# Norms of a two-phase transformer kernel: gated rows kept in PSUM, the last half block in two pieces, first features taken straight from the bank

## The chip, the cores and the metric

The kernel runs on one core of a Trainium2 chip. The metric is device microseconds of one execution, as the median of several runs. The names of the engines are those of the profile: PE is TensorE (matmul), DVE is VectorE, ACT is ScalarE, POOL is GpSimd, SP is SyncE, whose queue issues most DMAs.

## What is computed

Two transformer stacks run one behind the other on a batch of one with 256 tokens of width 1024, everything in fp32. The first has two layers on the tokens `x` and on a context `ctx` (its second layer needs the context for the scan's state alone). Cut to what the change touches:

```
for l in range(2):                                   # first stack
    ux = modulate(rmsnorm(x, norm1_g[l]), sh1, sc1) @ w_in[l]     # the same for ctx
    mix_x = concat(conformer_conv(ux), rwkv_out(scan(ux)))
    x = x + gt1 * (mix_x @ w_out[l])                 # gt1, gt2: rows of 1024 gates
    x = x + gt2 * swiglu(modulate(rmsnorm(x, norm2_g[l]), sh2, sc2), wg, wu, wd)
    # layer 0: ctx gets the same two steps
x = rmsnorm(x) * final_g
for l in range(2):                                   # second stack
    x = layer_norm(ALPHA * x + 0.5 * swiglu_2(x, ffn1_w13[l], ffn1_w2[l]))
    x = layer_norm(ALPHA * x + mixer(x))
    x = layer_norm(ALPHA * x + 0.5 * swiglu_2(x, ffn2_w13[l], ffn2_w2[l]))
```

## The kernel before

**Tiling.** Tokens lie on the partitions in two blocks of 128, `x[0]` and `x[1]` (written x0 and x1 in the order's rows), each with 1024 columns in SBUF. A product that ends in token-major form is accumulated in four PSUM banks `acc[b][h]` (acc00 to acc11), block b by half h of 512 columns. Matmuls of fp32 accuracy are made of three: data and weights are each kept as a rounded part and a remainder (`wh` and `wl` for weights, `hi` and `lo` for data), and hi·wh, hi·wl and lo·wh are added up. `wsplit` (L346) makes `wh` with a cast on ACT and `wl` with a subtraction on DVE (L341, L342). The first two weight tiles behind each norm are made apart from that: cast on ACT (L364), subtraction on POOL (L365), a `tensor_tensor` of 128x1024 that reads two SBUF tiles.

**Between two products stands a norm.** There are 11 places in which the PE has finished one product and needs the normalised result for the next:

- six in the first stack. `add_gated` multiplies each bank by a row of gates into an SBUF tile T2 (L620) and adds that to `x` (L621); `rms_blocks` squares each half on ACT with a running sum (L416), adds the two sums in a 128x1 instruction on DVE (L418), takes square root (ACT L384) and reciprocal (DVE L385), and scales (ACT L423, DVE L425). They lie at about 381, 683 (both on the context), 808, 1062, 1347 and 1554 us. At the last three nothing else is ready for the PE; at the first three the scan of the other stream and the gates of the next layer (`ada`) run beside it.
- five in the second stack, at about 1756, 1970, 2164, 2358 and 2577 us. `ln` adds ALPHA·x to the bank (DVE L1146), `ln_norm` takes statistics (L394), merges them (L396), and scales block 0 on ACT (L404) and block 1 on DVE (L406). A sixth LayerNorm ends the program.

Behind both, `feature_major` transposes the eight features of both blocks on the PE (L438), block 0 first, into four banks, and evacuates them by the list `EVAC`: "A e 0" is ACT taking feature 0 to an fp32 tile with scale and shift (L454; on DVE L456 and L458), "h" the cast to the rounded part (ACT L460), "l" the remainder (DVE or POOL, L462). The list fixes the order on each engine.

**What sets the order.** `down_last` gives the last tiles of a product (two in the first stack, four in the second) in three parts: all of block 0, then half 0, then half 1 of block 1, so that the norm of block 0 starts early. All else is put in order by a scheduler that simulates the program's time when it is built; it runs over the whole program, and its waits between engines are put in with it.

Of the kernel before, what the change touches and what calls it, by code (L numbers as in the profile page):

```python
# [47 lines left out]
HALF = [slice(0, 512), slice(512, 1024)]  # L48

# [118 lines left out]
def _layout(a):  # L168
# [84 lines left out]
    "A e 0,D e 2,A h 0,D l 0,A e 1,D e 3,A h 1,A h 2,D l 1,A h 3,D l 2,A e 4,D l 3,A h 4,D e 6,P l 4,A e 5,D e 7,"  # L253
    "A h 5,P l 5,A h 6,A h 7,D l 6,D l 7").split(",")]
# [4 lines left out]
class Prog:  # L259
# [128 lines left out]
    def ln_norm(self, x, b, pre):  # L388

        nc = self.nc  # L390
        st = self.tiny([P, 2, 6])
        for h in range(2):
            pre(b, h)
            nc.vector.bn_stats(st[:, h, :], x[:, HALF[h]])  # L394
# [14 lines left out]
    def rms_blocks(self, blocks, keep=False):  # L409
# [3 lines left out]
        ss = [self.tiny([P, 3]) for _ in range(2)]  # L413
        for b in range(2):
            for h in range(2):
                nc.scalar.activation(self.t(self.pool, [P, 512], "sq", bufs=1), blocks[b][:, HALF[h]], AF.Square,  # L416
                                     accum_out=ss[b][:, h : h + 1])
            nc.vector.tensor_add(ss[b][:, 2:3], ss[b][:, 0:1], ss[b][:, 1:2])  # L418
        for b in range(2):
            r = self.rstd_of(ss[b][:, 2:3], 1.0 / D, RMS_EPS, [P, 1])  # L420
# [7 lines left out]
    def feature_major(self, yb, scale, bias, perm=False, new=None, acc=True):  # L428
# [12 lines left out]
        for e, op, f in (EVAC if acc else EVAC1):  # L441
            hi, lo = hs[f // 4][:, f % 4, :], ls[f // 4][:, f % 4, :]
            eng = {"A": nc.scalar, "D": nc.vector, "P": nc.gpsimd}[e]
            with self.tc.issue_after(last[e].ins) if e in last and acc else contextlib.nullcontext():
                if op == "e":
                    ts[f] = t = self.T1([P, T])
# [88 lines left out]
    def down(self, acc, h, w, start, stop, parts=((0, 0), (0, 1), (1, 0), (1, 1))):  # L535

        for b in range(2):
            s = slice(b * P, b * P + P)
            ns = [n for b_, n in parts if b_ == b]
            for a, c in ((0, 0), (0, 1), (1, 0)):  # L540
                for n in ns:
                    last = self.mm(acc[b][n], h[a][:, s], w[c][:, HALF[n]], start and a == 0 and c == 0,
                                   stop and a == 1)
        return last

    def down_last(self, acc, args):
# [3 lines left out]
        for parts in (((0, 0), (0, 1)), ((1, 0),), ((1, 1),)):  # L550
# [63 lines left out]
    def add_gated(self, x, acc, row):  # L614
        nc = self.nc
        for b in range(2):
            for h in range(2):
                s = HALF[h]
                t = self.T2([P, 512])
                nc.vector.tensor_mul(t, acc[b][h], row[:, s])  # L620
                nc.vector.tensor_add(x[b][:, s], x[b][:, s], t)  # L621
# [518 lines left out]
    def ln(self, x, acc, l, i):  # L1140
# [3 lines left out]
        def pre(b, h):  # L1144
            s = HALF[h]
            nc.vector.scalar_tensor_tensor(x[b][:, s], x[b][:, s], ALPHA, acc[b][h], ALU.mult, ALU.add)  # L1146
# [492 lines left out]
```

## Time and profile before

| | us |
|---|---|
| median of 3 runs | 2779.92 |
| lowest, highest | 2776.57, 2785.88 |
| the profiled execution | 2783.58 |
| its span, first to last instruction | 2781.8 |

The mean granted clock of TensorE in the profiled execution is 0.959 of full speed. The PE is busy for 2632.1 us (95% of the span), DVE for 1716.4, ACT for 1327.3 and POOL for 670.2. What an edit at a norm can give is thus looked for in the PE's gaps, and in what ends each gap, not in the busy shares.

### The profile page before, as it was taken

What the parts mean: (1) busy time and instruction counts of PE and PEld (TensorE: products, weight loads), DVE (VectorE), ACT (ScalarE), POOL (GpSimd) and SP (SyncE); (2) the same over time, 40 slices, a digit from 0 to 9 for tenths busy, and PEclk for the clock granted to TensorE, in tenths of its full rate; (3) what the DMA queues carried; (4) which work ended last, traced back from release to release, by engine and by line L of the source; (5) the groups of instructions that cost most, each with busy time, mean ns of one, the idle gap of its engine ahead of it and who ended that gap; (6) DMA issues with size and microseconds to landing.
All of it is one profiled execution on the core that took longest, in us unless ns stands there. A gap on an engine that the chain in (4) does not pass through costs nothing.

```text
span 2781.8 us, 53780 instructions
## 1 busy us (share of the span) xinstructions
PE 2632.1 (95%) x22398; PEld 2291.3 (82%) x22398; DVE 1716.4 (62%) x2703; ACT 1327.3 (48%) x2015; POOL 670.2 (24%) x669
## 2 busy tenths in 40 slices
PE   7889989999889998899899899999999999999998
PEld 4866867888678896866699899889899898889897
DVE  3885778645577555984555655666655655755655
ACT  5523654434565346433544544654544544644543
POOL 0388999920130001384200000010000000100000
PEclk9989989999899999979899999999999999999999
DMA  7345425334323354234355555524555555425653
GB/s 250 109 145 175 147 84 180 132 130 157 117 77 116 136 182 144 95 137 153 117 187 185 194 183 188 193 87 156 182 187 185 182 188 174 166 83 182 205 184 120
DMA packets 118768, 430.71 MB, mean 155 GB/s; under 512 B 13174, under 2 KB 13686, under 8 KB 118524
## 3 DMA queue, kind: packets, MB, share of 16 engines
q1 hardware_dynamic: 118524, 427.28, 45.2%
q8 instruction: 175, 2.87, 0.4%
q14 instruction: 69, 0.57, 0.1%
HBM read 425.13 MB, written 2.10 MB: 154 GB/s over the span
## 4 chain that ended last, share of the span: by engine, by line
PE 78%; DVE 11%; ACT 4%; POOL 3%; issue 2%; DMA 2%; SPq 0%; ACTq 0%; DVEq 0%; POOLq 0%
PE pb L333 33%; PE acc L333 25%; PE ps L333 19%; DVE wl L342 3%; DVE T1c L726 1%; POOL tap L732 1%; DVE S L964 1%; DVE T L962 1%; DMA raw<-in_ada 1%; DVE x L621 1%; ACT wh L341 1%; POOL x L733 1%; PE acc L438 1%; DMA raw<-in_wr 0%; DVE T2b L620 0%
## 5 line engine op out<-in xcount | busy, mean ns | idle before, releaser
L342 DVE TENSOR_TENSOR wl<-raw,wh 128x1024 fp32r<-128x1024 f32 (+1 forms) x654 | 811.9, 1245 | 622.2 <-ACT wh L341 391.7
L341 ACT CAST wh<-raw 128x1024 fp32r<-128x1024 f32 (+1 forms) x654 | 681.9, 1046 | 892.3 <-PE pb L333 345.8
L333 PE MATMUL pb<-xf,wh 128*128 128x256 f32 (+1 forms) x2560 | 486.4, 289 | 12.6 <-ACT T1b L585 4.1
L333 PE MATMUL pb<-S,wh 128*128 128x256 f32 x2560 | 492.0, 289 | 4.8 <-DVE S L631 1.8
L333 PEld LDWEIGHTS pb<-xf,wh 128*128 128x128 f32 (+1 forms) x2560 | 409.8, 194 | 26.7 <-DVE T1b L588 6.6
L333 PEld LDWEIGHTS pb<-S,wh 128*128 128x128 f32 x2560 | 408.5, 192 | 22.4 <-issue 11.8
L333 PE MATMUL ps<-S,wh 128*128 128x256 f32 x2048 | 390.4, 287 | 0.6 <-ACT S L460 0.5
L333 PE MATMUL pb<-xf,wl 128*128 128x256 f32 (+1 forms) x1280 | 371.2, 291 | 8.7 <-DVE wl L342 8.7
L365 POOL TENSOR_TENSOR wl<-raw,wh 128x1024 fp32r<-128x1024 f32 x22 | 54.9, 2504 | 1340.4 <-ACT wh L364 826.9
L333 PE MATMUL pb<-S,wl 128*128 128x256 f32 x1280 | 367.4, 287 | 2.0 <-DVE wl L342 2.0
L333 PEld LDWEIGHTS ps<-S,wh 128*128 128x128 f32 x2048 | 326.8, 192 | 9.0 <-issue 3.4
L333 PE MATMUL ps<-S,wl 128*128 128x256 f32 x1024 | 293.4, 286 | 0.6 <-DVE wl L342 0.6
L333 PEld LDWEIGHTS pb<-xf,wl 128*128 128x128 f32 (+1 forms) x1280 | 248.1, 194 | 16.7 <-DVE wl L342 11.5
L333 PEld LDWEIGHTS pb<-S,wl 128*128 128x128 f32 x1280 | 245.4, 192 | 6.6 <-issue 3.0
L333 PE MATMUL acc<-wh,T 128*128 128x512 f32 x704 | 206.3, 393 | 0.0
L333 PEld LDWEIGHTS ps<-S,wl 128*128 128x128 f32 x1024 | 196.7, 192 | 2.8 <-issue 1.4
L333 PE MATMUL acc<-wh,T1b 128*128 128x512 f32 x528 | 157.5, 396 | 3.5 <-ACT T1b L341 3.5
L732 POOL TENSOR_SCALAR tap<-z,cols 128x255 f32<-128x255 f32 (+14 forms) x120 | 149.2, 1252 | 0.0
L333 PEld LDWEIGHTS acc<-wh,T 128*128 128x128 f32 x704 | 126.9, 189 | 23.6
L732 POOL TENSOR_SCALAR tap<-x,cols 128x246 f32<-128x246 f32 (+6 forms) x104 | 111.4, 1079 | 46.1 <-DVE x L671 46.0
L733 POOL TENSOR_TENSOR x<-x,tap 128x247 f32<-128x247 f32 (+8 forms) x132 | 106.8, 809 | 34.4 <-ACT tap L730 28.0
L733 POOL TENSOR_TENSOR z<-z,tap 128x255 f32<-128x255 f32 (+14 forms) x120 | 112.8, 940 | 3.9
(445 smaller groups left out, 3968.7 us busy)
## 6 DMA issues: line engine op xcount, KB each, us to landing
raw<-in_fu SPq DMA_DIRECT2D x132, 512.0 KB, 3.2
raw<-in_ada SPq DMA_DIRECT2D x96, 512.0 KB, 4.3
raw<-in_pu SPq DMA_DIRECT2D x88, 512.0 KB, 4.2
raw<-in_qu SPq DMA_DIRECT2D x88, 512.0 KB, 3.7
raw<-in_fd SPq DMA_DIRECT2D x66, 512.0 KB, 3.2
raw<-in_wr SPq DMA_DIRECT2D x51, 512.0 KB, 3.6
raw<-in_pd SPq DMA_DIRECT2D x44, 512.0 KB, 4.1
raw<-in_qd SPq DMA_DIRECT2D x44, 512.0 KB, 3.8
```

Of the source, the lines that this page charges most:

```text
L333: return self.nc.tensor.matmul(out, lhsT, rhs, start=start, stop=stop, **kw)
L341: self.nc.scalar.copy(hi, src)
L342: self.nc.vector.tensor_sub(lo, src, hi.bitcast(F32))
L365: self.nc.gpsimd.tensor_sub(lo, r, hi.bitcast(F32))
L438: nc.tensor.transpose(pt[f // 2][:, f % 2, b, :], yb[b][:, f * P : f * P + P], self.cst("ident"))
L621: nc.vector.tensor_add(x[b][:, s], x[b][:, s], t)
L726: nc.vector.scalar_tensor_tensor(av[:, d], z[:, f, s], w(j), av[:, d], ALU.mult, ALU.add)
L732: nc.gpsimd.tensor_scalar(t[:, d], z[:, f, s], w(j), None, ALU.mult)
L733: nc.gpsimd.tensor_add(zc[f][:, d], zc[f][:, d], t[:, d])
L962: nc.vector.tensor_mul(tv, tj[:, k + 1 : 32, k : k + 1].broadcast_to([P, m, k + 1]), X[:, k : k + 1, 0 : k + 1].broadcast_to([P, m, k + 1]))
L964: nc.vector.tensor_sub(X[:, k + 1 : 32, 0 : k + 1], X[:, k + 1 : 32, 0 : k + 1], tv)
```

## The change

Three edits, of which two are in the norms and one in the evacuation.

1. `add_gated` multiplies the bank by the gates in place: the product stays in PSUM, and the add reads `x` from SBUF and the product from PSUM. The tile T2 is gone there.
2. `PIECES` divides the second half of block 1 in two pieces of 256 columns. `down_last` has four parts in place of three, and the matmuls of the last two are 256 columns wide; the gated add, ALPHA·x, the statistics (four of 256 for block 1) and the squares of block 1 follow the pieces. `rms_blocks` has three squares and two small sums for block 1.
3. `EVAC` has the new operation "H": ACT writes the rounded part of features 0 and 1 straight from the bank, while DVE takes the fp32 copy of the same feature. DVE has 12 operations in place of 10, ACT 11 in place of 12, POOL 1 in place of 2.

```diff
+PIECES = HALF, [slice(0, 512), slice(512, 768), slice(768, 1024)]
+
+
+def piece(acc, s):
+
+    return acc[s.start // 512][:, s.start % 512 : s.start % 512 + s.stop - s.start]
...
 EVAC = [t.split() for t in (
-    "A e 0,D e 2,A h 0,D l 0,A e 1,D e 3,A h 1,A h 2,D l 1,A h 3,D l 2,A e 4,D l 3,A h 4,D e 6,P l 4,A e 5,D e 7,"
-    "A h 5,P l 5,A h 6,A h 7,D l 6,D l 7").split(",")]
+    "A H 0,D e 0,D l 0,A H 1,D e 1,A e 2,D l 1,A h 2,D e 3,A h 3,D l 2,A e 4,D l 3,A h 4,D e 6,A e 5,D l 4,A h 5,D e 7,"
+    "P l 5,A h 6,D l 6,A h 7,D l 7").split(",")]
...
     def ln_norm(self, x, b, pre):
 
         nc = self.nc
-        st = self.tiny([P, 2, 6])
-        for h in range(2):
-            pre(b, h)
-            nc.vector.bn_stats(st[:, h, :], x[:, HALF[h]])
+        n = 2 * len(PIECES[b]) - 2
+        st = self.tiny([P, n, 6])
+        for s in PIECES[b]:
+            pre(b, s)
+            for q in range(s.start * n // D, s.stop * n // D):
+                nc.vector.bn_stats(st[:, q, :], x[:, D // n * q : D // n * (q + 1)])
...
-        ss = [self.tiny([P, 3]) for _ in range(2)]
+        ss = [self.tiny([P, 5]) for _ in range(2)]
+        sums = []
         for b in range(2):
-            for h in range(2):
-                nc.scalar.activation(self.t(self.pool, [P, 512], "sq", bufs=1), blocks[b][:, HALF[h]], AF.Square,
-                                     accum_out=ss[b][:, h : h + 1])
-            nc.vector.tensor_add(ss[b][:, 2:3], ss[b][:, 0:1], ss[b][:, 1:2])
+            c = lambda i: ss[b][:, i : i + 1]
+            for i, s in enumerate(PIECES[b]):
+                nc.scalar.activation(self.t(self.pool, [P, 512], "sq", bufs=1)[:, 0 : s.stop - s.start], blocks[b][:, s],
+                                     AF.Square, accum_out=c(i))
+                if i:
+                    nc.vector.tensor_add(c(2 + i), c(i), c(1 + i if i > 1 else 0))
+            sums.append(c(2 + i))
         for b in range(2):
-            r = self.rstd_of(ss[b][:, 2:3], 1.0 / D, RMS_EPS, [P, 1])
+            r = self.rstd_of(sums[b], 1.0 / D, RMS_EPS, [P, 1])
...
-                if op == "e":
-                    ts[f] = t = self.T1([P, T])
+                if op in "eH":
+
+                    t = hi
+                    if op == "e":
+                        ts[f] = t = self.T1([P, T])
...
             for a, c in ((0, 0), (0, 1), (1, 0)):
                 for n in ns:
-                    last = self.mm(acc[b][n], h[a][:, s], w[c][:, HALF[n]], start and a == 0 and c == 0,
-                                   stop and a == 1)
+                    last = self.mm(piece(acc[b], n), h[a][:, s], w[c][:, n], start and a == 0 and c == 0,
+                                   stop and a == 1 and n.stop % 512 == 0)
...
-        for parts in (((0, 0), (0, 1)), ((1, 0),), ((1, 1),)):
+        for parts in ([(0, s) for s in PIECES[0]], *([(1, s)] for s in PIECES[1])):
...
     def add_gated(self, x, acc, row):
         nc = self.nc
         for b in range(2):
-            for h in range(2):
-                s = HALF[h]
-                t = self.T2([P, 512])
-                nc.vector.tensor_mul(t, acc[b][h], row[:, s])
-                nc.vector.tensor_add(x[b][:, s], x[b][:, s], t)
+            for s in PIECES[b]:
+                a = piece(acc[b], s)
+                nc.vector.tensor_mul(a, a, row[:, s])
+                nc.vector.tensor_add(x[b][:, s], x[b][:, s], a)
...
-        def pre(b, h):
-            s = HALF[h]
-            nc.vector.scalar_tensor_tensor(x[b][:, s], x[b][:, s], ALPHA, acc[b][h], ALU.mult, ALU.add)
+        def pre(b, s):
+            nc.vector.scalar_tensor_tensor(x[b][:, s], x[b][:, s], ALPHA, piece(acc[b], s), ALU.mult, ALU.add)
```

The scheduler's simulation comes out otherwise, and with it the order of much of the first stack: before about 1380 us PE, DVE and ACT work of different streams changes places at many points. ACT's table loads are 83 in the order of the changed kernel, 79 in that before. Behind that point the order differs at the norms alone.

Three pieces of the order, in both kernels. The words in brackets name the engines on whose progress an instruction waits ("Activation" is ACT).

DVE at the final RMS norm (1554 us), from the first product of block 1 on; acc10 and acc11 are the halves of block 1, `tnb` are the 128x1 sums. Before:

```order
L620 TENSOR_TENSOR T2b_2960_17188<-acc10_2668_15285,Sb_2655_15254 128x512 [waits DVE_49,PE_49]
L620 TENSOR_TENSOR T2b_2961_17191<-acc11_2669_15286,Sb_2655_15254 128x512 [waits DVE_49,PE_49]
L621 TENSOR_TENSOR x1_68<-x1_68,T2b_2960_17188 128x512 [waits DVE_49]
L621 TENSOR_TENSOR x1_68<-x1_68,T2b_2961_17191 128x512 [waits DVE_49]
L418 TENSOR_TENSOR tnb_2962_17194<-tnb_2962_17194 128x1 [waits Activation_49]
L418 TENSOR_TENSOR tnb_2963_17195<-tnb_2963_17195 128x1 [waits Activation_49]
L385 RECIPROCAL tnb_2968_17206<-tnb_2968_17206 128x1 [waits Activation_49]
L385 RECIPROCAL tnb_2969_17211<-tnb_2969_17211 128x1 [waits Activation_49]
```

and changed:

```order
L636 TENSOR_TENSOR acc10_2655_15326<-acc10_2655_15326,Sb_2642_15295 128x512 [waits PE_49]
L636 TENSOR_TENSOR acc11_2656_15327<-acc11_2656_15327,Sb_2642_15295 128x256 [waits PE_49]
L637 TENSOR_TENSOR x1_68<-x1_68,acc10_2655_15326 128x512 [waits DVE_49]
L637 TENSOR_TENSOR x1_68<-x1_68,acc11_2656_15327 128x256 [waits DVE_49]
L431 TENSOR_TENSOR tnb_2945_17239<-tnb_2945_17239 128x1 [waits Activation_49]
L636 TENSOR_TENSOR acc11_2656_15327<-acc11_2656_15327,Sb_2642_15295 128x256 [waits DVE_49]
L637 TENSOR_TENSOR x1_68<-x1_68,acc11_2656_15327 128x256 [waits DVE_49]
L393 RECIPROCAL tnb_2952_17254<-tnb_2952_17254 128x1 [waits Activation_49]
L431 TENSOR_TENSOR tnb_2946_17240<-tnb_2946_17240 128x1 [waits Activation_49]
L431 TENSOR_TENSOR tnb_2946_17240<-tnb_2946_17240 128x1 [waits DVE_49,Activation_49]
```

The sums of block 0 come between the two pieces of acc11. The first piece of acc11 waits for the PE, the second waits for DVE alone.

ACT at the first LayerNorm (1756 us): S is the scaled block, `wh` the rounded part of the second of the two weight tiles that POOL finishes. Before:

```order
L384 ACTIVATE tn_19195<-tn_19193,const 128x1
L364 CAST wh_19312<-raw_19310 128x1024
L404 ACTIVATE S_19198<-x_67,tn_19199,tn_19195 128x512 x2
L384 ACTIVATE tn_19210<-tn_19208,const 128x1
L454 ACTIVATE T_3296_19240<-acc_3292_19220,cols 128x256
```

and changed:

```order
L392 ACTIVATE tn_19255<-tn_19253,const 128x1
L414 ACTIVATE S_19258<-x_67,tn_19259,tn_19255 128x512 x2
L372 CAST wh_19375<-raw_19373 128x1024
L392 ACTIVATE tn_19273<-tn_19271,const 128x1
L471 ACTIVATE S_19279<-acc_3276_19283,cols 128x256 x2
```

The cast of `wh` stands behind the scaling of block 0 instead of ahead of it; the first two evacuations are now the "H" ones.

DVE at the same norm, from ALPHA·x of block 1's first half on. Before:

```order
L1146 SCALAR_TENSOR_TENSOR x1_68<-x1_68,acc10_2990_17289 128x512 [waits PE_49]
L385 RECIPROCAL tn_3281_19195<-tn_3281_19195 128x1 [waits Activation_49]
L401 SCALAR_TENSOR_TENSOR tn_3283_19199<-tn_3280_19193,tn_3281_19195 128x1 [waits DVE_49]
L394 BN_STATS tn_3284_19203<-x1_68 128x6
L1146 SCALAR_TENSOR_TENSOR x1_68<-x1_68,acc11_2991_17290 128x512 [waits PE_49]
L394 BN_STATS tn_3284_19203<-x1_68 128x6 [waits DVE_49]
L396 BN_AGGR tn_3285_19208<-tn_3284_19203 128x2 [waits DVE_49]
L385 RECIPROCAL tn_3286_19210<-tn_3286_19210 128x1 [waits Activation_49]
L406 TENSOR_SCALAR S_3287_19213<-x1_68,tn_3285_19208,tn_3286_19210 128x512 [waits DVE_49]
L406 TENSOR_SCALAR S_3287_19213<-x1_68,tn_3285_19208,tn_3286_19210 128x512
```

and changed:

```order
L1161 SCALAR_TENSOR_TENSOR x1_68<-x1_68,acc10_2974_17337 128x512 [waits PE_49]
L393 RECIPROCAL tn_3265_19255<-tn_3265_19255 128x1 [waits Activation_49]
L411 SCALAR_TENSOR_TENSOR tn_3267_19259<-tn_3264_19253,tn_3265_19255 128x1 [waits DVE_49]
L404 BN_STATS tn_3268_19263<-x1_68 128x6 x2
L1161 SCALAR_TENSOR_TENSOR x1_68<-x1_68,acc11_2975_17338 128x256 [waits PE_49]
L1161 SCALAR_TENSOR_TENSOR x1_68<-x1_68,acc11_2975_17338 128x256
L404 BN_STATS tn_3268_19263<-x1_68 128x6 [waits DVE_49] x2
L406 BN_AGGR tn_3269_19271<-tn_3268_19263 128x2 [waits DVE_49]
L393 RECIPROCAL tn_3270_19273<-tn_3270_19273 128x1 [waits Activation_49]
L416 TENSOR_SCALAR S_3271_19276<-x1_68,tn_3269_19271,tn_3270_19273 128x512 [waits DVE_49]
L416 TENSOR_SCALAR S_3271_19276<-x1_68,tn_3269_19271,tn_3270_19273 128x512
```

Two steps of 256 columns stand in place of one of 512, and both stand ahead of the statistics of either; the second of them has no wait of its own.

## Rows read from the trace of the kernel before

**Rows 1.** Busy time of the first stack (stretch, us, busy per engine and instructions, PEclk granted clock).

```profile
0.00:1380.00 1380.00, 1268.87 (x12986) 1035.18 (x12987) 904.69 (x1549) 649.54 (x1077) 608.54 (x633) 0.93 0.41 139
```

**Rows 2.** The same view, three stretches around the final RMS norm.

```profile
1553.00:1557.45 4.45, 4.43 (x18) 3.29 (x18) 3.38 (x6) 1.08 (x3) 0.72 (x1) 1.00 0.19 75
1557.45:1567.75 10.30, 3.27 (x16) 3.27 (x17) 7.25 (x12) 6.56 (x17) 4.47 (x2) 0.75 0.36 116
1567.75:1580.00 12.25, 12.25 (x98) 12.25 (x98) 11.42 (x19) 9.61 (x17) 1.47 (x2) 0.93 0.62 219
```

**Rows 3.** Chain of waits around the final RMS norm (start us, us, what).

```profile
1558.16 4.31 DVE x L621 x2
```

**Rows 4.** Timeline of DVE there (start us, us, line, out<-in, count [idle before <-releaser]).

```profile
1555.66 1.28 DVE L621 TENSOR_TENSOR x<-x,T2b 128x512 f32<-128x512 f32 x2
...
1558.08 4.39 DVE L621 TENSOR_TENSOR x<-x,T2b 128x512 f32<-128x512 f32 x2
1562.39 0.15 DVE L418 TENSOR_TENSOR tnb<-tnb 128x1 f32<-128x1 f32 x1
```

**Rows 5.** Timeline of POOL there.

```profile
1556.73 5.19 POOL L365 TENSOR_TENSOR wl<-raw,wh 128x1024 fp32r<-128x1024 f32 x2 [190.24 <-PE acc L333]
```

**Rows 6.** Timeline of PE: the first transposes behind three RMS norms.

```profile
1072.61 3.67 PE L438 MATMUL acc<-const,S 128*128 128x128 f32 x16 [7.04 <-ACT S L423]
...
1358.93 3.67 PE L438 MATMUL acc<-const,Sb 128*128 128x128 f32 x16 [8.54 <-ACT Sb L423]
...
1564.48 3.68 PE L438 MATMUL acc<-const,x 128*128 128x128 f32 x16 [7.04 <-ACT x L423]
```

**Rows 7.** Timeline of ACT at the norm near 1347 us.

```profile
1356.34 1.28 ACT L384 ACT_TABLE_LOAD   x1
```

**Rows 8.** Timeline of DVE at the first LayerNorm.

```profile
1756.06 0.69 DVE L1146 SCALAR_TENSOR_TENSOR x<-x,acc 128x512 f32<-128x512 f32 x1 [1.22 <-PE acc L333]
1756.78 0.69 DVE L394 BATCH_NORM_STATS2 tn<-x 128x6 f32<-128x512 f32 x1
...
1758.28 1.00 DVE L406 TENSOR_SCALAR S<-x,tn,tn 128x512 f32<-128x512 f32 x2
...
1760.45 0.43 DVE L462 TENSOR_TENSOR S<-T,S 128x256 fp32r<-128x256 f32 x1 [0.33 <-ACT S L460]
```

**Rows 9.** Timeline of ACT there.

```profile
1754.02 1.05 ACT L364 CAST wh<-raw 128x1024 fp32r<-128x1024 f32 x1 [0.69 <-PE acc L333]
1754.97 1.52 ACT L404 ACTIVATE S<-x,tn,tn 128x512 f32<-128x512 f32 x2
...
1759.42 0.56 ACT L454 ACTIVATE T<-acc,cols 128x256 f32<-128x256 f32 x1 [1.37 <-PE acc L438]
1760.01 0.40 ACT L460 CAST S<-T 128x256 fp32r<-128x256 f32 x1
```

**Rows 10.** Timeline of POOL there.

```profile
1755.15 2.37 POOL L365 TENSOR_TENSOR wl<-raw,wh 128x1024 fp32r<-128x1024 f32 x1 [6.65 <-ACT wh L364]
```

**Rows 11.** Timeline of PE there.

```profile
1758.88 1.11 PE L438 MATMUL acc<-const,S 128*128 128x128 f32 x8 [1.64 <-DVE S L406]
1760.47 0.45 PE L333 MATMUL ps<-S,wh 128*128 128x256 f32 x1 [0.48 <-ACT S L460]
```

**Rows 12.** Timeline of DVE inside a mixer of the first stack.

```profile
1114.70 2.95 DVE L851 TENSOR_SCALAR S<-S,cols,omka 128x512 f32<-128x512 f32 x2
```

**Rows 13.** Timeline of POOL there.

```profile
1114.46 1.48 POOL L848 TENSOR_TENSOR S<-z,S 128x512 f32<-128x512 f32 x1
1115.90 5.13 POOL L852 TENSOR_TENSOR S<-S,S 128x512 f32<-128x512 f32 x3
```

**Rows 14.** Timeline of DVE at the context norm near 381 us.

```profile
387.19 0.68 DVE L418 TENSOR_TENSOR tnb<-tnb 128x1 f32<-128x1 f32 x1
```

**Rows 15.** Timeline of POOL there.

```profile
386.89 1.76 POOL L733 TENSOR_TENSOR z<-z,tap 128x247 f32<-128x247 f32 x2
```

**Rows 16.** Chain of waits at the norm near 808 us.

```profile
811.38 5.10 DVE x L621 x2
```

More of the change, by code (lines that the diff above doesn't have):

```diff
@@ L533, in accs, with down @@
         return [[self.pacc(2 * b + h) for h in range(2)] for b in range(2)]
-    def down(self, acc, h, w, start, stop, parts=((0, 0), (0, 1), (1, 0), (1, 1))):
+    def down(self, acc, h, w, start, stop, parts=tuple((b, s) for b in range(2) for s in HALF)):
         for b in range(2):
```

## Prediction

> **What bounds the kernel now.** I read the busy time by stretch first, then the gaps of the PE at the norms, then the engines inside a gap. The PE is busy for 1268.87 of the first 1380 us, nearly all of the first stack [rows 1], and so idle for 111. At the three last norms of the first stack that idle time stands in one piece: 7.04, 8.54 and 7.04 us before the first transposes, each ended by ACT's scaling [rows 6]. Inside the last one, from the end of the accumulation (1557.45) to the next matmul (1567.75), the PE does nothing but its 16 transposes, at a granted clock of 0.75 [rows 2]. The chain of waits shows what fills it: 4.31 us of two adds L621 [rows 3]. Two such adds took 1.28 us just before, and 4.39 us when POOL was at work on its two subtractions of 128x1024, 5.19 us from 1556.73 [rows 4, 5]. So the add, with two sources in SBUF, is held until a POOL instruction ends: the first of block 1's adds by the first subtraction, the second by the other. The multiplications, with a source in PSUM, are not: ALPHA·x at the LayerNorm, also PSUM and SBUF, takes 0.69 us while POOL works [rows 8, 10].
>
> At the LayerNorms the gap is shorter: ALPHA·x on the last half starts with the product's end at 1756.06, block 1's scaling at 1758.28, its transposes start at 1758.88 and the next matmul at 1760.47, which waited for ACT's cast [rows 8, 11].
>
> **Gated rows in PSUM: the three bare norms.** The step removes the hold on the adds. It leaves the small sums of the squares, 128x1 with both sources in SBUF: one of these took 0.68 us under a POOL add of 128x247 [rows 14, 15], where the one behind the pair takes 0.15 [rows 4]. I therefore let them be held as well. The order sets block 0's sum ahead of the second piece's multiplication, so DVE stands until the first subtraction ends, 1556.73 + 2.6 = 1559.3; multiplication and add of 256 columns follow (0.43 each, by a DVE instruction of that size [rows 8]) to 1560.2, the square to about 1560.9. Block 1's sums are then held until the second subtraction ends at 1561.92. From a sum to the scaled block took 1.2 us before (1562.47, the end of the adds, to 1564.48, less 0.8 of square), so block 1 is scaled at about 1563.2, where block 0's transposes are done. Its eight transposes take half of 3.68 us [rows 6]: 1565.0, against 1567.8. The gain is 2.8 us each at 1062 and 1554. At 1347 a table load of 1.28 us lies on the path before the square root [rows 7]; block 0's earlier square root now takes it while the others wait, and I add 0.5 of the 1.28: 3.3. Sum −8.9. Were the small sums not held, block 1 would be scaled at 1561.5 and the gain 4.5 each, 5.1 us more for the three.
>
> No row shows DVE writing to PSUM. The nearest is ALPHA·x, which reads PSUM, 0.69 us [rows 8]; 0.55, as the scaling without PSUM, and 1.4, twice as long, bound it. I take 0.69: between 1560.9 and 1561.92 lies a slack of 1 us, and even the upper bound for the last pieces eats less than that.
>
> The Trainium skill (SBUF — State Buffer, Who interferes with whom) says that a DVE instruction with two SBUF inputs contends with a POOL instruction that reads SBUF, one with at most one SBUF input outside the double-port modes does not, and the loser blocks for the whole instruction, whatever its size. By it the small sums are held and the three norms give 8.9; only the one row of 128x1 bears that out here.
>
> **The clock takes some back.** The granted clock is at its lower level, 1.2 of 2.4 GHz, for half of the stretch with the transposes (0.75) and 1.7 of the 12.25 us behind (0.93) [rows 2]. If that stretch stays where it is while matmuls start 2.8 us earlier, 2.8 us of matmuls run at half pace and 1.4 is lost at each norm; if it ends as much earlier, nothing. I take a quarter: +1.0 for the three, bounds 0 and +4.2.
>
> **The norms with work beside them.** At 808 the chain runs through two held adds, 5.10 us [rows 16]; free they take 1.28, so 3.8 come free on DVE. The scan's own DVE and PE steps stand behind them in the chain, so some of this is late anyway: −2.5, bounds 0 and −3.8. At 381 and 683 other work keeps the PE going: 0, bounds −1 and +1.
>
> **The two pieces.** The intent is that DVE starts on columns 512 to 768 while the PE still adds up the rest. The order says otherwise: the first piece waits for the PE, the second for nothing but DVE (or nothing at all). Both lie in one bank, so the wait of the first covers the last matmul of the bank, and it starts no sooner than the whole half did. At the LayerNorm two steps of 256 columns (0.43 each, overlapping by a tenth) and two statistics replace 0.69 + 0.69: about 0.1 later, bounds 0 and +0.4. On the PE 512 columns cost 0.246 us (18 in 4.43) and 256 columns 0.125 (98 in 12.25, some at the lower clock) [rows 2]: twice 12 narrow matmuls for 12 wide cost at most 0.1. For 11 places I take +0.5, bounds 0 and +2.
>
> **The LayerNorms: a new hold.** Before, ACT made the cast first (1754.02, 1.05 us), POOL's subtraction ran from 1755.15 for 2.37 us and ended at 1757.5, before block 1's scaling at 1758.28 [rows 8 to 10]. Now the order puts both scalings of block 0 ahead of the cast. They can't start before 1754.02, where ACT took up the cast; I give DVE's two small steps ahead of them 0.25 (an estimate), and they take 1.52 us: 1755.78; the cast ends at 1756.8, and POOL works from 1756.9 to 1759.25. Block 1's scaling on DVE, ready at 1758.4, falls into that. It is a `tensor_scalar` from SBUF to SBUF, with one source only, but such an instruction is held too: two of 128x512 took 2.95 us while POOL was on `tensor_tensor` [rows 12, 13], against 1.00 for two at the LayerNorm [rows 8]. So it ends at about 1759.5 (POOL's end and half of its own 0.55) instead of 1758.83: +0.7 at each of five norms. The cast has no other place on ACT's queue: what is queued behind it is block 1's square root, which needs the merged statistics and comes later anyway.
>
> **The evacuation.** Rounding feature 0 straight from the bank saves the 0.56 us of ACT's fp32 copy ahead of the 0.40 cast [rows 9] and makes the first matmul up to 0.4 earlier. DVE gets one copy more and one subtraction more, 0.54 + 0.43, at most 0.96 if the last features are late by all of it. At the two mixer-type norms, where the PE soon asks for all features, I take +0.3, at the three others −0.1; bounds −0.4 and +0.96 each. The five LayerNorms together: 3.5 + 0.3 = +3.8, with the pieces counted above.
>
> **Table loads and the rest of the order.** Four more loads of 1.28 us [rows 7]; I count one on the path, +1.3, bounds 0 and 5.1. For the new order of the first stack the trace has no price: 111 us of PE idle time [rows 1] could shrink or grow by a twentieth, ±5; I take 0.
>
> **Sum.** −8.9 + 1.0 − 2.5 + 0 + 0.5 + 3.8 + 1.3 = −4.8 on the profiled execution's 2783.58 us. That lay 3.66 above the median; I set the difference against the median: 2779.92 − 4.8 = 2775.1.
>
> **The rivals.**
> - *The sums and scalings are not held* (for: just one row for a 128x1 sum, and POOL may run elsewhere than I place it; against: the `tensor_scalar` rows). The three norms give 5.1 more, the LayerNorms 3.5 less loss: −13.4, 2766.5. If only the first of these holds, −9.9: 2770.0.
> - *The gain is given back behind the norm*: the half-clock stretch stays in place (+3.2 over what I took) and 808 is hidden: −4.8 + 3.2 + 2.5 = +0.9, 2780.8. For: after the final norm DVE is busy for 11.42 of 12.25 us [rows 2], so an earlier start meets a full engine.
> - *Slower: the first stack's new order starves the PE.* Its weights need ACT's cast and DVE's subtraction just in time, and the scan's steps share both engines; where those go first, the PE waits. It decides once the PE's 111 us of idle time grow by more than 13 us, an eighth: −4.8 + 15 = 2790. Against: all work there is the same but for the loads, and DVE loses the held time.
> - *The pieces are handed over early after all*: one step of 0.3 us at 11 places, −3.3: 2771.8, still a case of the forecast. The missing wait speaks against it.
>
> **How the numbers follow.** About 0.3% (8.3 us) is what a measurement of this kernel can tell from no change. The forecast, 2775.1, has 0.46 and its own range 2769 to 2781; not held 0.27 (three quarters of it beyond −8.3); given back 0.14; slower 0.13. Faster: 0.20 of the second, and 0.14 of the forecast's case where 808 pays in full and the order helps: 0.34. Slower 0.13, the rest 0.53. The range reaches from the first rival at a good order (2763) to just under the third (2787).
>
> **What would show it.** Right: the adds L637 at 0.7 us beside POOL; sums L431 ending with POOL's instructions; PE gaps of about 4 instead of 7.04; at the LayerNorms POOL's subtraction from 1756.9 of that time scale and L416 at 1.1 or more; the first piece starting at the last matmul's end. Wrong: L416 at 0.55, L431 at 0.16, or a PE idle time up to 1380 us that differs from 111 − 12 by more than 5.

## The result

The changed kernel takes 2805.02 us (median of 6 runs, 2800.78 to 2817.83) against 2783.54 for the kernel before in the same session: ratio 1.0087, interval 1.0062 to 1.0112, or 24 us slower by the ratio (the two medians lie 21.5 apart). The prediction was 2775.1 with a range to 2787, and gave slower 0.13.

Where the time went is read from one event that both kernels have 673 times in the same sequence, the start of the cast of a weight tile to its rounded part. The table gives how much later the k-th of them starts than in the profile of before. Each column is one profile, and profiles differ: ten of the kernels below have the instructions and the order of before up to 381 us, and at 330 they stand between -3.0 and +6.8, so steps of a few microseconds say nothing there. Between 1152 and 1288 the seven kernels that keep the first stack's order agree within 2 us (-0.5 to +1.2).

| before, us | the change | PSUM product alone | new order alone, late | new order alone, early |
|---|---|---|---|---|
| 330 | +10.5 | -0.3 | +0.6 | +6.2 |
| 653 | +9.9 | +0.7 | +0.6 | +6.8 |
| 859 | +14.7 | -3.1 | +4.2 | +5.7 |
| 1055 | +14.3 | -0.2 | +7.1 | +5.7 |
| 1152 | +16.1 | -3.9 | +9.4 | +5.1 |
| 1288 | +14.0 | -4.4 | +14.5 | +14.9 |
| 1388 | +15.2 | -8.1 | +14.2 | +8.6 |
| 1736 | +13.3 | -9.2 | +14.2 | +8.9 |
| 2025 | +21.6 | -6.9 | +14.1 | +12.0 |
| 2757 | +26.3 | -9.5 | +11.7 | +10.5 |

The change is 10.5 us behind at 330, before the first norm whose gated add or evacuation list it changes. The kernel with the pieces alone has the same instructions in the same order up to 381 us and is 2.1 behind there, so most of the 10.5 is the difference of one profile from another. At 1388 the change is some 15 behind, and in the second stack it loses 13 more; this is rough too, since a kernel whose second stack is that of before (the list at one norm, below) loses 6.6 behind 1736 in its profile. Between 1388 and 1736, where the final RMS norm lies and the order is that of before, it gains 1.9.

The PE's gaps at the bare norms (the three at which nothing else is ready for the PE) did what was forecast. The timeline of the PE at 1062, 1347 and 1554 us of before (here some 12 to 16 us later), which answers to [rows 6]:

```profile
1085.58 3.67 PE L452 MATMUL acc<-const,S 128*128 128x128 f32 x16 [4.11 <-ACT S L437]
...
1374.44 3.27 PE L452 MATMUL acc<-const,Sb 128*128 128x128 f32 x16 [5.37 <-ACT Sb L437]
...
1576.90 3.67 PE L452 MATMUL acc<-const,x 128*128 128x128 f32 x16 [4.20 <-ACT x L437]
```

The idle times are 4.11, 5.37 and 4.20 us instead of 7.04, 8.54 and 7.04. The timelines of DVE and of POOL at the last of them, which answer to [rows 4, 5]:

```profile
1573.09 1.01 DVE L637 TENSOR_TENSOR x<-x,acc 128x512 f32<-128x512 f32 x2
1574.13 0.70 DVE L431 TENSOR_TENSOR tnb<-tnb 128x1 f32<-128x1 f32 x1
1574.76 0.42 DVE L636 TENSOR_TENSOR acc<-acc,Sb 128x256 f32<-128x256 f32 x1
...
1575.62 1.78 DVE L431 TENSOR_TENSOR tnb<-tnb 128x1 f32<-128x1 f32 x2
```

```profile
1572.46 4.66 POOL L373 TENSOR_TENSOR wl<-raw,wh 128x1024 fp32r<-128x1024 f32 x2 [188.69 <-PE acc L341]
```

The adds L637 run beside POOL at their free pace (two, of 512 and 256 columns, in 1.01 us). The sum of block 0 takes 0.70 us and the two of block 1 take 1.78: the first of these ends at 1577.14, with POOL's pair (1577.12), and the second 0.26 behind it.

The shorter gaps don't arrive as time: in the rows from 1055 to 1152 and from 1288 to 1388, in which the norms at 1062 and 1347 lie, the change loses 1.8 and 1.2 us, while the PSUM product alone gains 3.7 and 3.7.

At the first LayerNorm, DVE, ACT, POOL and PE of the changed kernel (the answer to [rows 8 to 11]):

```profile
1769.45 0.75 DVE L1161 SCALAR_TENSOR_TENSOR x<-x,acc 128x256 f32<-128x256 f32 x2 [1.25 <-PE acc L341]
...
1771.73 1.47 DVE L416 TENSOR_SCALAR S<-x,tn,tn 128x512 f32<-128x512 f32 x2
1773.87 0.54 DVE L475 TENSOR_SCALAR T<-acc,cols 128x256 f32<-128x256 f32 x1 [0.68 <-ACT S L471]
...
1775.05 0.54 DVE L475 TENSOR_SCALAR T<-acc,cols 128x256 f32<-128x256 f32 x1 [0.17 <-ACT S L471]
```

```profile
1769.00 1.03 ACT L372 CAST wh<-raw 128x1024 fp32r<-128x1024 f32 x1
...
1773.27 0.56 ACT L471 ACTIVATE S<-acc,cols 128x256 fp32r<-128x256 f32 x1 [1.78 <-PE acc L452]
1774.45 0.56 ACT L471 ACTIVATE S<-acc,cols 128x256 fp32r<-128x256 f32 x1 [0.61 <-DVE T L475]
```

```profile
1770.11 2.34 POOL L373 TENSOR_TENSOR wl<-raw,wh 128x1024 fp32r<-128x1024 f32 x1 [8.31 <-ACT wh L372]
```

```profile
1772.80 1.72 PE L452 MATMUL acc<-const,S 128*128 128x128 f32 x8 [2.03 <-DVE S L416]
1774.17 0.56 PE L341 MATMUL ps<-S,wh 128*128 128x256 f32 x1
1774.93 0.58 PE L341 MATMUL ps<-S,wh 128*128 128x256 f32 x1 [0.20 <-DVE S L479]
```

ACT casts behind the scaling of block 0; POOL then works from 1770.11 for 2.34 us, and the scaling of block 1 (L416, two in 1.47 us instead of 1.00) is held. The PE's wait is 2.03 instead of 1.64. Behind it something stands that the prediction did not have: DVE's copy of feature 0 (L475) was idle 0.68 us until ACT's rounding of it ended, ACT's rounding of feature 1 was idle 0.61 until DVE's copy ended, and DVE's next copy waited for ACT again. The two engines take turns on the bank that features 0 and 1 share. Before, DVE's first copy there was of feature 2, in another bank; it waited for the PE and ran beside ACT's copy of feature 0 (1759.42 in [rows 9]):

```profile
1759.58 0.54 DVE L458 TENSOR_SCALAR T<-acc,cols 128x256 f32<-128x256 f32 x1 [0.30 <-PE acc L438]
```

### The profile page after: what moved, and what is told of

Its sections match the earlier page's. It is cut to its first block, busy times and chain, and to the rows that moved or that the text cites. A ratio compares the mean times of both kernels' runs of the same rounds, so it can differ in the third digit from the quotient of the medians.

```text
span 2808.6 us, 54045 instructions
## 1 busy us (share of the span) xinstructions
PE 2645.1 (94%) x22506; PEld 2311.2 (82%) x22506; DVE 1728.3 (62%) x2763; ACT 1333.9 (47%) x2024; POOL 654.7 (23%) x658
## 4 chain that ended last, share of the span: by engine, by line
PE 76%; DVE 12%; ACT 5%; issue 2%; DMA 2%; POOL 2%; SPq 0%; DVEq 0%; ACTq 0%; POOLq 0%
PE pb L341 31%; PE acc L341 25%; PE ps L341 19%; DVE wl L350 2%; DVE T1c L742 1%; DMA raw<-in_ada 1%; DVE S L980 1%; DVE T L978 1%; ACT wh L349 1%; POOL tap L748 1%; POOL x L749 1%; DMA raw<-in_wr 0%; PE acc L452 0%; ACT L392 0%; DVE acc L636 0%
## 5 line engine op out<-in xcount | busy, mean ns | idle before, releaser
L341 PEld LDWEIGHTS pb<-xf,wl 128*128 128x128 f32 (+1 forms) x1280 | 247.3, 193 | 13.3 <-DVE wl L350 9.0
L341 PE MATMUL acc<-wh,T 128*128 128x512 f32 (+1 forms) x736 | 207.6, 383 | 0.0
L341 PEld LDWEIGHTS acc<-wh,T1b 128*128 128x128 f32 x540 | 97.7, 192 | 22.4 <-ACT T1b L349 4.4
L341 PE MATMUL acc<-wl,T 128*128 128x512 f32 (+1 forms) x368 | 115.9, 385 | 0.0
```

Source lines behind the costliest of these rows:

```text
L341: return self.nc.tensor.matmul(out, lhsT, rhs, start=start, stop=stop, **kw)
```

## Experiments

**One edit at a time.** The kernel before with one of the three edits each: `t = acc[b][h]` in place of the tile T2; the pieces alone; the list alone.

```diff
-                t = self.T2([P, 512])
+                t = acc[b][h]
```

> The kernel before with the gated product kept in PSUM alone, in halves of 512 as before; the order of all instructions is otherwise that of the kernel before. If the loss of the full change comes from the pieces and the new evacuation list, this kernel is faster than before by 8 to 13 us: the PE's gaps in front of the transposes at 1062, 1347 and 1554 us fall from 7.04, 8.54 and 7.04 to about 4.2, 5.4 and 4.2 (as in the changed kernel), and 808 gives 1 to 4. If writing PSUM from DVE is what costs (the rival), this kernel is no faster, and the multiplications L620 last well over 0.7 us.

Measured: ratio 0.9970 (0.9955 to 0.9985), 8.4 us faster. Its multiplications into PSUM and its adds run at 0.65 us each; the timelines of DVE and the PE at 1554 us:

```profile
1546.98 1.30 DVE L620 TENSOR_TENSOR acc<-acc,Sb 128x512 f32<-128x512 f32 x2 [1.71 <-PE acc L333]
1548.18 1.28 DVE L621 TENSOR_TENSOR x<-x,acc 128x512 f32<-128x512 f32 x2
...
1552.72 2.21 DVE L418 TENSOR_TENSOR tnb<-tnb 128x1 f32<-128x1 f32 x2
```

```profile
1556.20 1.11 PE L438 MATMUL acc<-const,x 128*128 128x128 f32 x4 [5.32 <-ACT x L423]
```

The total is as expected, the gaps are not: 5.24, 5.54 and 5.32, some 1.1 us longer than in the full change at two of the norms. Without pieces the first 128x1 sum (L418) came when POOL had just begun its second subtraction, and the two sums took 2.21 us; over the program (line L418, its count and shortest, median and longest duration in ns) one of these sums took 2140:

```profile
L418 DVE TENSOR_TENSOR tnb<-tnb x12: 141/154/2140, 111.9 to 1554.8; 128x1 f32<-128x1 f32 x12
```

Behind 808 the kernel was 3.1 us ahead (at 859) and at 930 no longer: that norm gave nothing. The five other kernels with the PSUM product and the first stack's order of before show the same two steps, 2.7 to 4.0 us gained by 859 and 2.8 or 2.9 lost again by 930.

> The pieces alone: gated product through SBUF and the old evacuation list. Theory: slower by 8 to 18 us, most of it before 1065 us, where the order of the first stack is new; at each LayerNorm +0.4 to +0.8, because the cast now stands behind the scaling and DVE's scaling of block 1 is held by POOL (1.47 us for two instead of 1.00). Rival, that the new evacuation list does all the harm: within 3 us of before.

Measured: 1.0090 (1.0060 to 1.0120), 25 us slower, more than expected. Its profile is of the fastest of its four runs, 8.7 us below their median, and shows only 15.4 us: 7.5 by 1055, 4.3 more by 1388, 2.1 at the final norm, and 1.5 behind. ACT makes 83 table loads in it and in the full change, 79 in before and in the kernel with the list alone.

> The new evacuation list alone. Theory: ACT and DVE take turns on the bank that features 0 and 1 share, so the first remainder comes later and the last one too; +0.8 to +1.3 us at each of five LayerNorms, 4 to 7 in the second stack, and anything between -3 and +10 in the first stack, whose order is new too. Rival, that the pieces do all the harm: within 2 us of before in the second stack.

Measured: 1.0083 (1.0057 to 1.0108), 23 us slower. In its profile 22.1 us were lost by 1388 (expected at most 10), 17.5 of them between 1152 and 1288; 5.0 behind 1600, as expected.

The three effects, -8.4, +25 and +23, add up to 40, not to 24: some of what the pieces and the list cost must be one thing that both set off. The scheduler's order of the first stack is the candidate, since the PSUM product alone leaves all orders as they were, and the two others don't.

**The full change without the pieces.**

```diff
-PIECES = HALF, [slice(0, 512), slice(512, 768), slice(768, 1024)]
+PIECES = HALF, HALF
```

> The full change without the pieces: gated product in PSUM and the new list everywhere. The scheduler gives the first stack nearly the order of the list alone. If the effects add up, list alone +23 and PSUM product -8.5, it is 14 to 15 us slower than before, 6 to 8 faster than the full change; the LayerNorms cost 5 to 6 together, less than half of the full change's 13. If the pieces are what makes the full change slow, it is within 3 us of before.

Measured: 1.0049 (1.0033 to 1.0065), 13.6 us slower: list and PSUM product do add up, and the pieces on top of them cost some 11 us (1.0087 less 1.0049), not 25. The gaps at the three bare norms are 5.24, 5.54 and 5.30 us, as with the PSUM product alone, so it is the pieces that shorten two of them by another 1.1 us in the full change.

**The edits in the second stack alone, the first stack's order kept.** The list by itself, and then, with the PSUM product everywhere, both pieces and list.

```diff
...
-        for e, op, f in (EVAC if acc else EVAC1):
+        for e, op, f in ((EVAC2 if self.tags is TAGS2 else EVAC) if acc else EVAC1):
...
```

EVAC2 is the new list there, EVAC the old one.

> The new evacuation list in the second stack alone (the six places behind 1554 us); the order of the first stack is that of before. Theory: nothing up to 1554 us (within 1 us), then +0.8 to +1.3 us at each of the LayerNorms and at the final RMS norm, total +4 to +8. If the harm of the list comes only through a new order of the first stack, within 1 us of before.

Measured: 1.0015 (1.0001 to 1.0030), 4.2 us slower; its profile lost 5.6 behind 1554 us. ACT and the PE at the third LayerNorm:

```profile
2169.03 0.56 ACT L460 ACTIVATE S<-acc,cols 128x256 fp32r<-128x256 f32 x1 [1.31 <-PE acc L441]
2170.20 0.56 ACT L460 ACTIVATE S<-acc,cols 128x256 fp32r<-128x256 f32 x1 [0.61 <-DVE T L464]
```

```profile
2169.64 0.38 PE L336 MATMUL ps<-S,wh 128*128 128x256 f32 x1
2169.87 0.28 PE L336 MATMUL pb<-S,wh 128*128 128x256 f32 x1
2170.68 0.58 PE L336 MATMUL ps<-S,wh 128*128 128x256 f32 x1 [0.54 <-DVE S L468]
```

The first matmul is 0.5 us earlier than with the old list (1.09 us behind the first transpose of block 1, in [rows 11] 1.59), and the third then waits 0.54 for the remainder. From the first transpose of block 1 to the 49th matmul behind the eight transposes, the five LayerNorms together take 49.7 us with this list and 44.0 in the kernel with the PSUM product and the old list.

> Gated product in PSUM everywhere, pieces and new evacuation list in the second stack alone. The first stack's order is then that of before. Theory: the new order of the first stack cost about 24 of the full change's loss (15 measured at 1388 us plus the 8 to 9 that the PSUM product gives), so up to 1554 us this kernel is 8 to 9 us ahead of before, like the PSUM product alone; behind it the pair of pieces and list costs 11 to 13 us as in the full change, total +2 to +5, within 0.3% of before. If pieces and list cost by themselves and not by order, the rival, the second stack would show it no larger than 7 (list 5.6 and pieces 1.5 measured singly), total -2.

Measured: 1.0001 (0.9986 to 1.0017), no difference from before: less than the +2 to +5 of the theory, more than the rival's -2. Its profile is 8.3 us ahead at 1388, as expected, and loses 12.9 behind 1736, of which the ratios bear out 8.6. So pieces and list, put into the first stack, cost the full change some 24 us there (1.0087 less 1.0001; in the profiles 15.2 behind instead of 8.3 ahead), and into the second about 8.6 (1.0001 less 0.9970).

**The list at one norm, and one subtraction at one norm.** Both edits touch the norm at 381 us alone.

> The new evacuation list at the first norm (381 us) alone, one place of eleven. By the place itself +1 us. Theory (order): +8 to +22 us, spread over the stretch to 1390 us and not at 381. Rival (the list's own cost): within 2 us of before.

Measured: 1.0037 (1.0025 to 1.0049), 10 us slower. Its profile is within 2.2 us of before up to 1152 (0.2 there), and loses 10.5 between 1152 and 1288. Busy time and clock of the same work there, before:

```profile
1151.70:1288.00 136.30, 124.52 (x1602) 92.10 (x1601) 101.99 (x213) 44.97 (x78) 101.79 (x114) 0.85 0.45 159
```

and with the list at one norm:

```profile
1151.90:1298.70 146.80, 131.25 (x1633) 94.46 (x1633) 101.06 (x211) 44.87 (x79) 101.13 (x114) 0.81 0.43 146
```

10.5 us longer, with 6.7 more of PE busy time (31 more matmuls fall into it, and the granted clock is 0.81 instead of 0.85) and 3.8 more idle: no norm lies in that stretch, and the kernel differs there from before in the order alone.

The other edit, cut from the list of that norm:

```diff
...
-D e 6,P l 4,A e 5
+D e 6,D l 4,A e 5
...
```

> The kernel before with one edit that costs next to nothing where it stands: at the first norm (381 us) alone, the remainder of feature 4 is subtracted on DVE instead of POOL (0.43 instead of 0.73 us). The scheduler then orders some 650 matmuls of the first stack otherwise. If any other order of the first stack is worse than that of before (theory), this kernel is slower by 8 to 22 us, none of it behind 1390 us. If the losses of the full change come from its own instructions (rival), it is within 2 us of before.

Measured: 0.9988 (0.9971 to 1.0006), no difference. The theory as it was put, that any other order is worse, falls.

**The order alone.** Nothing but the scheduler's priority of one norm is raised; matmuls, DVE and POOL instructions are those of before, and ACT has two table loads fewer in the early kernel. Early is the norm of `x` at about 120 us, late that of the context at 683; the edit of the late one:

```diff
-        cf = self.norm1(1, self.x, 1, False, self.Sr, acc=True)
+        with self.tc.high_priority():
+            cf = self.norm1(1, self.x, 1, False, self.Sr, acc=True)
```

> The kernel before with not one instruction of PE, DVE or POOL more or less: the norm of x (at about 120 us) is given a higher priority in the scheduler, and some 520 matmuls and 140 DVE instructions of the first stack come in another order (two table loads fewer). Theory (an order of the first stack costs or gives up to 20 us by itself): a difference of more than 4 us from before, slower more likely, all of it before 1390 us. Rival (only added work costs): within 3 us of before.

> The kernel before with the same instructions; the norm of the context in front of layer 1 (683 us) has a higher priority, which reorders 271 matmuls and 114 DVE instructions behind about 690 us. Theory (order): the stretch from 1150 to 1290 us, which was 10.4 us longer in the kernel with the list at one norm and 17.5 longer with the list everywhere, is longer by 3 or more here too; total between 0 and +15. Rival: within 3 us of before in every stretch.

Measured: 1.0040 (1.0025 to 1.0055) and 1.0044 (1.0029 to 1.0058), 11 and 12 us slower with the same instructions (the early one as expected, by more than 4; the late one within its 0 to 15, and its stretch from 1152 to 1288 is 5.1 longer, where 3 or more was expected). The first stack up to the same event, for before, the early and the late one, and the full change:

```profile
0.00:1387.80 1387.80, 1276.67 (x13043) 1042.57 (x13044) 908.60 (x1553) 652.66 (x1082) 608.54 (x633) 0.93 0.41 139
```

```profile
0.00:1396.40 1396.40, 1276.27 (x13043) 1039.38 (x13044) 911.18 (x1553) 649.75 (x1079) 603.11 (x633) 0.93 0.42 138
```

```profile
0.00:1402.00 1402.00, 1287.91 (x13043) 1049.32 (x13044) 909.57 (x1553) 652.87 (x1081) 607.15 (x633) 0.92 0.41 138
```

```profile
0.00:1403.00 1403.00, 1282.03 (x13073) 1052.24 (x13074) 911.58 (x1580) 659.07 (x1094) 598.20 (x628) 0.92 0.40 137
```

and for the kernel that has pieces and list in the second stack alone, and so the first stack's order of before:

```profile
0.00:1379.50 1379.50, 1272.81 (x13043) 1040.78 (x13044) 904.91 (x1553) 652.57 (x1082) 605.57 (x633) 0.94 0.42 140
```

All of the first three have 13043 matmuls. The early one has 9.0 us more of idle time on the PE (1396.4 - 1276.27 = 120.1, before 111.1) and the same busy time; the late one has 11.2 more of busy time, its granted clock being lower, and 3.0 more idle. The full change has 9.8 more idle, although the gaps at 1062 and 1347 are 6.1 shorter, and 5.4 more busy. Against the last line it has 14.3 more idle and 9.2 more busy: that is what it loses in the first stack by pieces and list.

The idle time is the steadier of the two. Up to this event it is 110 to 111 us in the two kernels that have the first stack of before, 105 to 107 in the six with the PSUM product and that order, and 114 to 122 in all eight with another order; 114.5 in the kernel with one subtraction moved, which was no slower. Busy time varies by 6 us among the kernels of one order. The granted clock of all runs, though, bears out a part of it: its mean is 0.9541 over the 10 runs of the late order and 0.9559 over the 7 of the early one, beside 0.9593 over the 24 of before. A straight line through those 24 gives 1.5 us for 0.001 of clock, so by this estimate 7 or 8 of the late order's 12 us go with the lower clock, and 5 of the early one's 11.

**Turns on the bank.** PSUM product everywhere; in the second stack a list in which ACT takes both reads of feature 0.

```diff
...
+    "A H 0,D e 2,A e 0,D l 0,A e 1,D e 3,A h 1,A h 2,..."
...
```

> Gated product in PSUM, and in the second stack a list in which ACT takes both the rounded part of feature 0 and its fp32 copy, one behind the other, so that ACT and DVE don't take turns on one bank; POOL keeps its two subtractions; no pieces. Theory (taking turns is what made the new list slow): no loss against the PSUM product alone at the LayerNorms, within -2 to +1 us of it, so 8 to 11 us faster than before. Rival (rounding from the bank is itself slow): 3 to 6 us slower than the PSUM product alone.

Measured: 0.9963 (0.9949 to 0.9976), 10.3 us faster than before. ACT and the PE at the third LayerNorm:

```profile
2161.93 0.56 ACT L460 ACTIVATE S<-acc,cols 128x256 fp32r<-128x256 f32 x1 [1.31 <-PE acc L441]
2162.40 1.01 ACT L460 ACTIVATE T<-acc,cols 128x256 f32<-128x256 f32 x2
```

```profile
2163.47 0.39 PE L336 MATMUL ps<-S,wh 128*128 128x256 f32 x1 [0.42 <-DVE S L468]
```

ACT reads the bank three times in a row without a wait; a wait of 0.42 us for DVE's remainder is left. The stretch of the five LayerNorms that took 49.7 us with the turns takes 44.0, as with the old list. Against the PSUM product alone the difference is within the intervals.

**Pieces with either list**, second stack alone, PSUM product everywhere.

> Gated product in PSUM everywhere, pieces in the second stack alone, old evacuation list. The first stack's order is that of before. Theory: the hold on DVE's scaling costs 0.4 to 0.7 us at each LayerNorm, 2 to 4 in all over the PSUM product alone, so 4 to 7 us faster than before. If pieces cost nothing without the list: 8 to 9 faster, like the PSUM product alone.

> As the kernel with PSUM product and pieces in the second stack, with the list in which ACT takes both reads of feature 0 (no turns on a bank). Theory (hold and turns are separate costs): the same 2 to 4 us over the same-engine list without pieces, so 5 to 8 faster than before, and 5 or more faster than the same kernel with the new list (which was equal to before). Rival (the pieces' hold is what the pair pays for): within 2 us of before.

Measured: 0.9976 (0.9967 to 0.9985) and 0.9977 (0.9965 to 0.9990), 6.7 and 6.4 us faster than before. DVE in the second of them, third LayerNorm:

```profile
2163.45 1.48 DVE L420 TENSOR_SCALAR S<-x,tn,tn 128x512 f32<-128x512 f32 x2
```

The scaling is held (1.48 for two) though there are no turns, and the PE's waits are 2.04 to 2.06 instead of 1.64 at all five. So the pieces cost 1.7 us over the old list and 3.9 over the same-engine one (five waits longer by 0.4 make 2.0), the new list 4.2, and the pair 8.6: whether the pair costs more than the sum of 6 can't be told at these intervals.

**The small sums.** The kernel with the same-engine list, with the sums of two norms (1347 and 1554) on ACT.

```diff
...
-            nc.vector.tensor_add(ss[b][:, 2:3], ss[b][:, 0:1], ss[b][:, 1:2])
...
+                nc.scalar.activation(ss[b][:, 2:3], ss[b][:, 1:2], AF.Identity, bias=ss[b][:, 0:1])
...
```

> The kernel with the gated product in PSUM and the same-engine list in the second stack, in which the small sums of the squares at the two norms at 1347 and 1554 us are made on ACT (one 128x1 instruction with a bias) instead of DVE. In the PSUM-only kernel such a sum took 2.14 us, held by POOL. Theory (the small sums are the next thing that is held): the gap in front of the transposes falls from 5.5 and 5.3 us to about 3.5 to 4, total 2 to 4 us faster than that kernel and 11 to 14 faster than before. Rival (POOL's second subtraction sets the end anyway, through the weights): gap unchanged.

Measured: 0.9959 (0.9943 to 0.9974), 11.4 us faster than before, the fastest of all, though only 1.1 us ahead of the one without it (expected 2 to 4) and not clear of it. At the final norm:

```profile
1550.84 0.29 ACT L422 ACTIVATE tnb<-tnb 128x1 f32<-128x1 f32 x1
```

```profile
1553.31 0.94 PE L444 MATMUL acc<-const,x 128*128 128x128 f32 x5 [3.55 <-ACT x L429]
```

The gap is 3.55 instead of 5.30 us, as expected; at 1347 it is 5.12 instead of 5.54, where 3.5 to 4 was expected: a table load of 1.28 us stands there on ACT between block 0's sum and its square root.

## Why the prediction was wrong

The loss adds up from three ratios: -8.4 us for the PSUM product, +8.6 for pieces and list in the second stack, and some +24 for pieces and list in the first. The forecast's terms for these were -10.4 (-8.9 and -2.5 and the clock's +1.0), +4.3 (LayerNorms and pieces), and 0, with 1.3 for one table load.

- **The bare norms: right in the gaps.** 4.11, 5.37 and 4.20 us against a forecast of about 4 and a gain of 2.8, 3.3 and 2.8 (measured 2.93, 3.17, 2.84). The mechanism was as told: the adds freed, the small sums held until POOL's subtractions end, DVE writing PSUM at the price of reading it. The first rival, that sums and scalings are not held, falls with the sums at 0.70 and 1.78 us and the scalings at 1.47. A 128x1 sum that took 2.14 us alone is the row that was missing; it was issued 0.23 us behind a POOL subtraction and ended with it. That agrees with the Trainium skill (SBUF — State Buffer, Who interferes with whom), by which the order of issue and not the shape of the operation decides who is blocked. The PSUM product alone gave 8.4; in the full change the time of these gaps is lost again within the stretches at 1062 and 1347.
- **808: wrong, small.** Forecast -2.5; the six kernels with the PSUM product and the old order gained about that by 859 and had lost it again at 930, as the second rival said of 808. That rival's other half, the clock behind the norms (+1.0 in the sum), did not show where the order was kept: at 1062, 1347 and 1554 the PSUM product alone gained 8.5 us (3.7, 3.7 and 1.1) for gaps that are 6.5 shorter.
- **The pieces: right in the order's reading.** The first piece starts at the last matmul's end (DVE's steps follow it at 1769.45 in one go); the hold on block 1's scaling was forecast at +0.7 per LayerNorm and is +0.4. That the pieces would shorten two of the bare norms by 1.1 us, through the place of a small sum, was in the sum only unknowingly.
- **The evacuation: a step that failed.** It was costed by counts of instructions per engine (+0.3 at two norms and -0.1 at three). The list alternates two engines on one bank, and the program makes them wait for each other; measured +4.2 in the second stack. The lists showed it before any run: before the change DVE's first copy takes feature 2, in another bank than ACT's feature 0; behind it the same feature and bank. The prediction reasoned from the bank for the pieces ("Both lie in one bank") and did not ask the same of the list. The Trainium skill (PSUM — Partial Sum Buffer, PSUM bank collisions raise a hardware error) asks for guarding by bank, not by address, reads included. The waits in the trace are the program's; no run here lets two engines read one bank at once.
- **The new order of the first stack: the step that decided.** The prediction said that "the trace has no price", wrote "±5; I take 0", and this term was mis-sized. Measured: some +24 where pieces and list enter the first stack, +11 and +12 for two orders with the same instructions, nothing for a third (one subtraction moved), +10 for the list at one norm. The third rival named this mechanism and put its price at 15, but its chance at 0.13: the argument against it, that all work is the same, carries nothing, since the same work in another order is just what costs. The lower clock, which the rival did not count, is a part of it. The prediction's own sign, a PE idle time up to 1380 us that differs from 111 - 12 by more than 5, came: 121 us. (The 12 there takes in the final norm, which lies behind 1380; without it the sum has some 9, and the sign comes all the same.)
- **Table loads.** The four more loads are in the trace. No run gives their price; as an estimate, four of 1.28 us [rows 7] are 5 us at most, and only kernels with the pieces in the first stack have them. The early order has two loads fewer than before and is 11 us slower.

That the 24 us are order and not the edits' own cost at the norms of the first stack is shown in part only: order alone costs about half of it in two cases, and the loss in the kernel with the list at one norm falls where only the order differs. As an estimate, the list, at 4.2 us for its six places behind 1554 us, would cost some 3.5 at the five of the first stack, where it lost 22; for the pieces, with their table loads, the share is more open. The full change with the first stack in the order of before wasn't tried. Why one order is better than another is open too; in both forms it is the PE's idle time and the clock, not one wait.

## What to carry to other kernels

Where a scheduler orders the work, an edit that changes the order of a tuned program should be priced by what other orders with the same work cost, and split into a part that keeps the order and one that doesn't: here the PSUM product, which keeps it, gives 8.4 us, and the rest takes 33, some 24 of them in the first stack. Profiles of one order can differ by several microseconds at one event, so a loss is placed by what several kernels share. A list that spreads reads over engines must be read by bank: here two engines on one bank took turns, and it cost 4.2 us. An instruction's size says nothing of how long it is held; a 128x1 sum can be the last thing that a norm waits for.

## What the runs showed of the hardware

- A 128x1 DVE add of two SBUF operands took 2.14 us beside a POOL subtraction, 0.15 without.
- DVE writes PSUM in place at the price of reading it: two multiplications of 128x512 in 1.30 us, of 256 columns 0.42.
- The same 13043 matmuls took 11.2 us more of PE busy time in another order, the granted clock up to that point being 0.92 instead of 0.93. In the 24 runs of the kernel before that were taken beside it the clock lay between 0.954 and 0.962, and the time went up by some 1.5 us for each 0.001 less (a straight line through them).
